# A two-layer trunk on one Trainium2 core: four block products of the up projection in wide matmuls, one more low part by DMA, and another order in the tail

## The chip, the cores and the metric

The kernel runs on one core of one Trainium2 chip. The metric is the device time of one execution in microseconds (us). A core has TensorE (PE, the matrix unit; PEld is its weight load), VectorE (DVE), ScalarE (ACT), GpSimd (POOL) and SyncE (SP), each with its own instruction queue that runs in order, and DMA engines that move data beside them. SP issues the loads of the weights; POOL issues the DMAs that add into their destination.

## The reference

The part that matters is the gated ConvFFN, which each of the two layers has. SEQ is 512, D_MODEL 1024, D_FF 2816, all in float32.

```python
def gated_conv_ffn(x, w_gate, w_up, conv_w, conv_b, w_down):
    g = jnp.einsum('bsd,df->bsf', x, w_gate)
    g = causal_dwconv3(g, conv_w) + conv_b
    up = jnp.einsum('bsd,df->bsf', x, w_up)
    return jnp.einsum('bsf,fd->bsd', jax.nn.silu(g) * up, w_down)
...
def reference(x, ...):
    h = x
    for layer in range(DEPTH):
        xn = rms_norm(h, norm_mix[layer])
        ...
        hn = rms_norm(h, norm_ffn[layer])
        h = h + gated_conv_ffn(hn, w_ffn_gate[layer], w_ffn_up[layer], conv_ffn[layer],
                               b_conv_ffn[layer], w_ffn_down[layer])
    return rms_norm(h, final_norm)
```

## The kernel before

**Two parts for each number.** Every float32 operand of a matmul is split into a high part and a low part of a faster matmul type (float32r): high is a copy on ACT, low is the operand minus high. A product takes three matmuls: high times high, high times low, low times high. There are two ways to make a low part. One is a subtraction on DVE (`parts` and `halves`, L150/L151 and L726/L727). The other (`summed`, L140 to L144, and L766 to L768) writes the negated operand with ACT, then has POOL issue a DMA that adds the operand to it, so that DVE is not used.

**The ConvFFN in pairs.** D_FF is 22 tiles of 128 columns. Tiles 0 and 1 are computed directly; then come ten pairs, f = 2, 4, ..., 20, in each of the two layers (`hidden`, `steps`, STEPS). The pair's gate (g) and up (u) projections are each a 2x2 block product of weights (halves of D_MODEL by two tiles) and activations (halves of the sequence), done in seven block products in place of eight. `prepare(f)` makes the weight sums and splits them: s12 (for products 5 and 6), s34 (for 7 and 3), the plain blocks for 1, 2 and 4. `products(f)` then runs the fourteen block products in the order g1, u1, g5, g2, g6, u5, u6, u2, g7, u7, g3, u3, g4, u4, and takes each result out of PSUM in `after`. Each of g and u has three PSUM banks in a pair: "a" for products 1, 6, 7 and 4 in turn, "e" for 5 and 3, "b" for 2 (BANK). A bank takes the next product only when the one before it has been read.

**Narrow and wide products.** A block product is 128 weight columns by 256 positions over 512 inputs (four steps `kp`). Narrow (L577): twelve matmuls of 256 columns, three a step, all into the left half of the bank. Wide (L567 and L570): high and low part of the activations lie side by side, four matmuls of 512 columns multiply the weight's high part with both at once, so that the low part's share lands in the bank's right half; four of 256 columns then add the weight's low part to the left half. The result is the sum of the two halves. `after` copies the left half with ACT (L806) and adds the right half on DVE (`add`, L794), or adds both halves on DVE where it accumulates. FIRST_WIDE is 6: for f = 6 to 20 all g products and u products 2, 5 and 3 are wide. `in_both` decides it.

**Down projection.** Between the pairs runs the down projection of earlier tiles (`half_down`, matmuls at L155 to L157), whose weights `parts` splits (whi_d on ACT, wlo_d on DVE in layer 0, whi_dn and wlo_dn in layer 1). In layer 1, the last four tiles (18 to 21) go through seven block products of their own, the tail: `block` splits activation blocks into `hg` buffers (high on ACT L1229/L1233, low on DVE L1230/L1234), `put` splits weights, `product` runs the matmuls (L1272) and `taken` adds the result to the output rows y on DVE (L1172). There products 1, 6, 7 (and 4) share a bank, "a", with one bank for each of two row blocks i: `taken(6, 0)` cannot start its matmuls before the addition of `taken(1, 0)` has read that bank.

**What sets the order.** The kernel is traced in program order and a scheduler orders the instructions of each engine by its own estimates, but `behind(x, y)` puts x after y, and `inorder` keeps those instructions that it marks in program order. Buffers of a pool are taken in turn, so an instruction can also wait for the last reader of the buffer that it is about to overwrite.

Of the kernel before, what the change touches and what calls it, by code (L numbers as in the profile page):

```python
# [8 lines left out]
F32 = mybir.dt.float32  # L9
# [22 lines left out]
def tile_trunk(ctx: ExitStack, tc: tile.TileContext, x, norm_mix, norm_ffn, final_norm,  # L32
# [555 lines left out]
    class Ffn:  # L588
# [140 lines left out]
        def prepare(self, f):  # L729

            layer, ap, n = self.layer, self.ap, f"{self.layer}_{f}"
            raws = ffn_weights(layer, f, [(key, half) for half in range(2) for key in "gu"])
            stat = {}

            def put(key, product, hi_lo, i):
                stat[key, product] = hi_lo[0][:, i], hi_lo[1][:, i]

            w = self.unit(f"a11_{n}")
            for i, key in enumerate("gu"):
                self.halves(w[0][:, i], w[1][:, i], raws[key, 0][0][:, :, :P])  # L740
                put(key, 1, w, i)
            for key in "gu":
                r0, r1 = raws[key, 0][0], raws[key, 1][0]
                s12, s34 = (ap.tile([P, 2, 4, P], F32, tag="sum", bufs=3, name=f"{x}{key}_{n}")
                            for x in ("s12", "s34"))
                behind(nc.vector.tensor_tensor(s12[:, 0], r0[:, :, P:], r1[:, :, P:], ALU.add),
                       self.added[key])
                nc.vector.tensor_tensor(s12[:, 1], s12[:, 0], r0[:, :, :P], ALU.subtract)
                w = self.unit(f"s12{key}_{n}")

                def split_s12():
                    self.halves(*w, s12)

                hi, lo = summed(*raws[key, 1], between=split_s12,
                                after=self.first_sums if f == 2 else None)
                put(key, 5, w, 0)
                put(key, 6, w, 1)
                behind(nc.vector.tensor_tensor(s34[:, 0], r0[:, :, :P], r0[:, :, P:],
                                               ALU.subtract), self.added[key])
                nc.vector.tensor_tensor(s34[:, 1], r1[:, :, :P], s12[:, 1], ALU.subtract)  # L760
                for i, product in enumerate((2, 4)):
                    c = slice(i * P, (i + 1) * P)
                    stat[key, product] = hi[:, :, c], lo[:, :, c]
                w = self.unit(f"s34{key}_{n}")
                if key == "g" and f >= FIRST_WIDE:
                    nc.scalar.activation(w[1], s34, AF.Copy, scale=-1.0)  # L766
                    nc.gpsimd.dma_start(w[1], s34, accum_op=ALU.add)
                    nc.scalar.activation(w[0], s34, AF.Copy)  # L768
                else:
                    self.halves(*w, s34)  # L770
                put(key, 7, w, 0)
                put(key, 3, w, 1)
            return stat

        def products(self, f, stat):

            layer, ap, n = self.layer, self.ap, f"{self.layer}_{f}"
            banks = {"g": {}, "u": {}}
            kept = ap.tile([P, 3, HALF], F32, tag="kept", bufs=1, name=f"kept{n}")
            pads = [padded_tile() for _ in range(2)]  # L780
            lo, hi = slice(2, 2 + HALF), slice(2 + HALF, 2 + S)
            dst = {("g", 1): pads[0][:, lo], ("g", 6): pads[0][:, hi], ("g", 7): pads[1][:, hi],
                   ("g", 4): pads[1][:, lo]}
            dst.update({("u", product): kept[:, i, :] for i, product in enumerate((1, 6, 7))})
            onto = {2: 1, 7: 7, 3: 6}
            s = {}

            def in_both(key, product):
                return f >= FIRST_WIDE and (key == "g" or product in (2, 5, 3))

            def add(d, bank, halves):
                ins = None
                for half in halves:
                    ins = nc.vector.tensor_tensor(d, bank[:, half * HALF : (half + 1) * HALF], d,  # L794
                                                  ALU.add)
                return ins

            def after(key, product, bank):
                halves = range(1 + in_both(key, product))
                if product in onto:  # L800
                    ins = add(dst[key, onto[product]], bank, halves)
                    if product == 7:
                        self.added[key] = ins
                elif (key, product) != ("u", 4):
                    d = dst[key, 7 if product == 5 else product]
                    nc.scalar.copy(d, bank[:, :HALF])  # L806
                    add(d, bank, halves[1:])

            for key, product in (("g", 1), ("u", 1), ("g", 5), ("g", 2), ("g", 6), ("u", 5),
                                 ("u", 6), ("u", 2), ("g", 7), ("u", 7), ("g", 3), ("u", 3),  # L810
                                 ("g", 4), ("u", 4)):
                bank = self.multiply(banks[key], f"{key}{n}", product, stat[key, product],
                                     in_both(key, product))
                after(key, product, bank)
                if (key, product) in (("g", 4), ("g", 3)):
                    j = product == 4
                    row = pads[j][:, 2:]
                    nc.vector.tensor_tensor(row, row, self.r, ALU.mult)  # L818
                    s[j] = self.silu(self.conv(pads[j], f + j), f + j)
                    if j and layer == 0:  # L820
                        nc.vector.tensor_tensor(s[1], s[1], self.r, ALU.mult)
            nc.vector.tensor_tensor(s[1][:, HALF:], kept[:, 2, :], s[1][:, HALF:], ALU.mult)
            nc.vector.tensor_tensor(s[1][:, :HALF], bank, s[1][:, :HALF], ALU.mult)
            if layer == 0:
                nc.vector.tensor_tensor(kept[:, :2, :], kept[:, :2, :],
                                        self.r.rearrange("p (a b) -> p a b", a=2), ALU.mult)
            s0 = s[0].rearrange("p (a b) -> p a b", a=2)
            nc.vector.tensor_tensor(s0, kept[:, :2, :], s0, ALU.mult)
            return [(f + 1, s[1]), (f, s[0])]

        def hidden(self, f, before=lambda i, j: None):
# [312 lines left out]
    def ffn1(norm):  # L1144
        with tc.tile_pool(name="f1", bufs=1) as ap:
# [56 lines left out]
            t1, t2 = (ap.tile([P, 2, S], F32, tag="sum", bufs=3, name=f"dnt{i}") for i in (1, 2))  # L1202
            stat = {}

            def put(product, how, src):
                stat[product] = how(src, 2, 512, f"dnp{product}")

            def less(dst, x, y_):
                behind(nc.vector.tensor_tensor(dst, x, y_, ALU.subtract), ffn.added["u"])
# [8 lines left out]
            put(3, summed, b22)  # L1218
            put(7, summed, b12)
            less(b21, b21, t2)  # L1220
            put(4, summed, b21)

            blocks = {}

            def block(product, n, srcs):
                hi, lo = (x.rearrange("p (a b) -> p a b", a=2) for x in hg[n])
                blocks[product] = hi, lo
                if not isinstance(srcs, list):
                    nc.scalar.activation(hi, srcs, AF.Copy)  # L1229
                    nc.vector.tensor_tensor(lo, srcs, hi.bitcast(F32), ALU.subtract)  # L1230
                    return None
                for i, src in enumerate(srcs):
                    ins = nc.scalar.activation(hi[:, i], src, AF.Copy)  # L1233
                    nc.vector.tensor_tensor(lo[:, i], src, hi[:, i].bitcast(F32), ALU.subtract)  # L1234
                return ins

            a11, a12 = ([rows[a + 2 * i + n][:, :HALF] for n in range(2)] for i in range(2))
# [6 lines left out]
            block(5, 4, s1)  # L1244
            for n in range(2):
                nc.vector.tensor_tensor(s2[:, n], s1[:, n], a11[n], ALU.subtract)
            block(6, 5, s2)
            for n in range(2):
                nc.vector.tensor_tensor(a12[n], a12[n], s2[:, n], ALU.subtract)
            last_split = block(3, 6, a12)  # L1250
            for n in range(2):
                nc.vector.tensor_tensor(a21[n], a11[n], a21[n], ALU.subtract)
            block(7, 2, a21)
            block(4, 3, a22)

            first_root = work("sd", 1, "first")
            behind(nc.scalar.activation(first_root, eps, AF.Sqrt), last_split)
            banks = {}

            def product(p, i, c0=0, c1=512, bank=None):  # L1260
# [8 lines left out]
                for k in range(2):  # L1269
                    for l, r, end in ((l_hi, r_hi, False), (l_hi, r_lo, False),  # L1270
                                      (l_lo, r_hi, k == 1)):
                        nc.tensor.matmul(ps, l[:, k, cs], r[:, k, c0:c1], start=first, stop=end,  # L1272
                                         skip_group_check=True)
                        first = False
                return ps

# [4 lines left out]
            def taken(p, i, cs, bank=None):  # L1281

                t = i + 2 * (p in (5, 7, 4))
                part = cs if bank else slice(0, 512)
                inorder(add(y[t][:, cs], product(p, i, part.start, part.stop, bank), t))

            def squared(t, cs):
                sq = tp.tile([P, S], F32, tag="sq", name=f"sqf{t}_{cs.start}")
# [25 lines left out]
                queue.dma_start(out[t * P : (t + 1) * P, cs], dst)  # L1314


            taken(1, 0, left)
            taken(1, 1, left)
            taken(2, 0, left)
            taken(5, 0, right)  # L1320
# [92 lines left out]
```

## Time and profile before

| | us |
|---|---|
| runs | 978.46 to 979.29, median 979.26 |
| profiled execution, its own time | 978.92 |
| its span, first to last instruction | 977.2 |
| busy PE, DVE, ACT, POOL | 966.7, 808.6, 575.6, 130.7 |

The profile is one execution, recorded by the hardware. A page gives busy times and shares of the span, the span in 40 slices (each digit is a share in tenths, PEclk is the granted clock of TensorE), and the chain of work that ended last. A row of a timeline has the start in us, the time that its instructions took together, engine, line, operation, output and inputs by the program's names, the shape, the count, and, in brackets, how long the engine sat idle before it and what ended that. Instructions of one engine overlap at their ends, so a step is read from start to start.

### The profile page before, as it was taken

The numbers are of one execution on the slowest core, as the hardware profiler recorded it, in microseconds if no ns is written. First come the engines' busy times: TensorE is split into PE (matmuls) and PEld (weight loads), VectorE is DVE, ScalarE is ACT, GpSimd is POOL, SyncE is SP. The second block draws the span as 40 slices with busy tenths as digits, with TensorE's granted clock in tenths as the row PEclk, the third lists the DMA queues.
The fourth block names the chain that finished last, engine by engine and source line by source line (L and its number), as shares of the span: only waits on it lengthen the run. The fifth ranks groups of instructions, "written<-read, shape, count | busy, mean of one in ns | idle before, by whom it ended". The sixth has DMA issues, their size and how long they took to land.

```text
span 977.2 us, 14496 instructions
## 1 busy us (share of the span) xinstructions
PE 966.7 (99%) x5456; PEld 845.6 (87%) x5456; DVE 808.6 (83%) x1331; ACT 575.6 (59%) x867; POOL 130.7 (13%) x151
## 2 busy tenths in 40 slices
PE   9999999999999999999999999999999999999996
PEld 7888888998888888888889988889988888888885
DVE  5887459999899898998887765499998979888887
ACT  5523347675565565654588734586665566555675
POOL 2141023010011000110310001310110011000122
PEclk9999999999999999999999999999999999999998
DMA  7442226555666475664324523265656566565674
GB/s 250 146 138 86 87 87 135 138 151 160 153 165 156 119 185 151 159 161 135 114 58 132 195 66 105 55 142 137 177 148 163 152 159 160 142 166 151 174 158 121
DMA packets 91249, 137.63 MB, mean 141 GB/s; under 512 B 4804, under 2 KB 59820, under 8 KB 91180
## 3 DMA queue, kind: packets, MB, share of 16 engines
q1 hardware_dynamic: 78316, 98.69, 30.8%
q0 software_dynamic: 11088, 36.18, 20.9%
q10 hardware_dynamic: 1776, 1.84, 0.6%
q8 instruction: 43, 0.70, 0.3%
q14 instruction: 26, 0.21, 0.1%
HBM read 98.42 MB, written 2.10 MB: 103 GB/s over the span
## 4 chain that ended last, share of the span: by engine, by line
PE 97%; DVE 2%; issue 0%; DMA 0%; ACT 0%; POOLq 0%; DVEq 0%; POOL 0%
PE d L155 3%; PE d L156 3%; PE d L157 3%; PE dn L155 3%; PE dn L156 3%; PE dn L157 3%; PE gu L155 2%; PE gu L157 1%; PE oo L157 1%; PE oo L156 1%; PE gu L156 1%; PE oe L157 1%; PE oe L155 1%; PE oo L155 1%; PE oe L156 1%; PE u_4a L577 1%
## 5 line engine op out<-in xcount | busy, mean ns | idle before, releaser
L612 DVE SCALAR_TENSOR_TENSOR c<-rows,prm,c 128x512 f32<-128x512 f32 x88 | 65.4, 746 | 0.7 <-ACT c L610 0.7
L142 POOL DMA_DIRECT2D wlo_g<-raw_g x20 | 17.2, 862 | 336.6 <-ACT rows L806 242.0
L155 PE MATMUL d<-a_hi,whi_d 128*128 128x512 f32 x144 | 56.1, 390 | 0.0
L155 PE MATMUL dn<-whi_dn,a_hi 128*128 128x512 f32 x144 | 56.1, 390 | 0.0
L156 PE MATMUL d<-a_lo,whi_d 128*128 128x512 f32 x144 | 56.1, 390 | 0.0
L156 PE MATMUL dn<-wlo_dn,a_hi 128*128 128x512 f32 x144 | 56.1, 390 | 0.0
L157 PE MATMUL d<-a_hi,wlo_d 128*128 128x512 f32 x144 | 56.0, 389 | 0.0
L157 PE MATMUL dn<-whi_dn,a_lo 128*128 128x512 f32 x144 | 56.0, 389 | 0.0
L620 ACT ACTIVATE s<-c,prm 128x512 f32<-128x512 f32 x44 | 31.6, 722 | 30.4 <-DVE c L612 30.4
L726 ACT ACTIVATE whi_a<-raw_g 128x512 fp32r<-128x512 f32 x20 | 12.6, 631 | 57.3 <-PE g_6e L567 7.9
L610 ACT ACTIVATE c<-rows,prm 128x512 f32<-128x512 f32 x44 | 31.6, 720 | 11.7 <-DVE rows L818 11.7
L211 POOL TENSOR_TENSOR ssq_f<-ssq_f,sq_f 128x512 f32<-128x512 f32 x14 | 19.8, 1412 | 135.4 <-ACT sq_f L210 100.5
L200 ACT ACTIVATE hg<-h,prm 128x512 fp32r<-128x512 f32 x24 | 17.3, 722 | 32.1 <-DVE h L313 32.1
L727 DVE TENSOR_TENSOR wlo_s34u<-s34u,whi_s34u 128x1024 fp32r<-128x1024 f32 x20 | 24.5, 1225 | 12.7 <-ACT whi_s34u L726 7.4
L151 DVE TENSOR_TENSOR wlo_dn<-raw_dn,whi_dn 128x1024 fp32r<-128x1024 f32 x18 | 22.0, 1224 | 14.2 <-ACT whi_dn L150 14.0
L151 DVE TENSOR_TENSOR wlo_d<-raw_d,whi_d 128x1024 fp32r<-128x1024 f32 x18 | 22.0, 1224 | 13.8 <-ACT whi_d L150 13.8
L157 PEld LDWEIGHTS dn<-whi_dn,a_lo 128*128 128x128 f32 x144 | 27.0, 188 | 5.7
L157 PEld LDWEIGHTS d<-a_hi,wlo_d 128*128 128x128 f32 x144 | 27.0, 188 | 5.7
L726 ACT ACTIVATE whi_s12g<-s12g 128x1024 fp32r<-128x1024 f32 x20 | 21.2, 1061 | 18.0 <-PE g_4e L577 8.7
L201 DVE SCALAR_TENSOR_TENSOR hg<-h,prm,hg 128x512 fp32r<-128x512 f32 x24 | 22.1, 921 | 11.7 <-ACT hg L200 11.7
L155 PEld LDWEIGHTS d<-a_hi,whi_d 128*128 128x128 f32 x144 | 27.1, 188 | 5.4
L155 PEld LDWEIGHTS dn<-whi_dn,a_hi 128*128 128x128 f32 x144 | 27.1, 188 | 5.3
(1125 smaller groups left out, 3398.7 us busy)
## 6 DMA issues: line engine op xcount, KB each, us to landing
raw_g<-in_w_ffn_gate_dram SPq DMA_DIRECT2D x40, 512.0 KB, 4.4
raw_u<-in_w_ffn_up_dram SPq DMA_DIRECT2D x40, 512.0 KB, 3.6
raw_dn<-in_w_ffn_down_dram SPq DMA_DIRECT2D x22, 512.0 KB, 3.6
wlo_u<-raw_u POOLq DMA_DIRECT2D x21, 512.0 KB, 7.2
wlo_g<-raw_g POOLq DMA_DIRECT2D x20, 512.0 KB, 4.7
raw_d<-in_w_ffn_down_dram SPq DMA_DIRECT2D x18, 512.0 KB, 3.5
wlo_s34g<-s34g POOLq DMA_DIRECT2D x16, 512.0 KB, 5.9
raw_oe<-in_w_out_even_dram SPq DMA_DIRECT2D x8, 512.0 KB, 3.5
```

Source lines behind the costliest of these rows:

```text
L151: behind(nc.vector.tensor_tensor(lo, raw, hi.bitcast(F32), ALU.subtract), after[0])
L155: nc.tensor.matmul(ps, lhs[0], rhs[0], start=start, stop=False)
L156: nc.tensor.matmul(ps, lhs[0], rhs[1], start=False, stop=False)
L157: nc.tensor.matmul(ps, lhs[1], rhs[0], start=False, stop=stop)
L200: nc.scalar.activation(hg[k][0], h[k], AF.Copy, scale=g)
L201: nc.vector.scalar_tensor_tensor(hg[k][1], h[k], g, hg[k][0].bitcast(F32), op0=ALU.mult, op1=ALU.subtract)
L211: nc.gpsimd.tensor_tensor(self.ssq, self.ssq, sq, ALU.add)
L610: nc.scalar.activation(c, t[:, 0:S], AF.Copy, scale=prm("cf", ft))
L612: nc.vector.scalar_tensor_tensor(c, t[:, i : S + i], prm("cf", i * NF + ft), c, op0=ALU.mult, op1=ALU.add)
L620: nc.scalar.activation(s, c, AF.Silu, bias=self.prm("bf", ft))
L726: nc.scalar.activation(hi, src, AF.Copy)
L727: nc.vector.tensor_tensor(lo, src, hi.bitcast(F32), ALU.subtract)
```

## The change

Three things change.

All u products of the pairs f = 6 to 20 are wide, as g's were: `in_both` no longer looks at key and product. Products 1, 6, 7 and 4 of u so get a right half that has to be added: for 1, 6 and 7 after the copy or with the accumulation, for 4 by a copy into `kept[:, 0]` and an addition, ahead of the final multiplication, which moves behind the one for s[0].

The low part of s12 for g in the same pairs is made by negated copy and DMA, as s34's was, in place of a subtraction on DVE (`split`).

In the tail of layer 1 the addition of the first product (`first_add`) stands in program order ahead of the blocks 3, 7 and 4, whose low splits are put behind it; the weight split of product 4 comes behind block 6; and the matmuls of `product` are kept in program order.

```diff
+                by_dma = key == "g" and f >= FIRST_WIDE
+
+                def split(w, src):
+                    if not by_dma:
+                        return self.halves(*w, src)
+                    nc.scalar.activation(w[1], src, AF.Copy, scale=-1.0)
+                    nc.gpsimd.dma_start(w[1], src, accum_op=ALU.add)
+                    nc.scalar.activation(w[0], src, AF.Copy)
+
                 def split_s12():
-                    self.halves(*w, s12)
+                    split(w, s12)
...
-                if key == "g" and f >= FIRST_WIDE:
-                    nc.scalar.activation(w[1], s34, AF.Copy, scale=-1.0)
-                    nc.gpsimd.dma_start(w[1], s34, accum_op=ALU.add)
-                    nc.scalar.activation(w[0], s34, AF.Copy)
-                else:
-                    self.halves(*w, s34)
+                split(w, s34)
...
             def in_both(key, product):
-                return f >= FIRST_WIDE and (key == "g" or product in (2, 5, 3))
+                return f >= FIRST_WIDE
...
-            nc.vector.tensor_tensor(s[1][:, HALF:], kept[:, 2, :], s[1][:, HALF:], ALU.mult)
-            nc.vector.tensor_tensor(s[1][:, :HALF], bank, s[1][:, :HALF], ALU.mult)
             if layer == 0:
                 nc.vector.tensor_tensor(kept[:, :2, :], kept[:, :2, :],
                                         self.r.rearrange("p (a b) -> p a b", a=2), ALU.mult)
             s0 = s[0].rearrange("p (a b) -> p a b", a=2)
             nc.vector.tensor_tensor(s0, kept[:, :2, :], s0, ALU.mult)
+            nc.vector.tensor_tensor(s[1][:, HALF:], kept[:, 2, :], s[1][:, HALF:], ALU.mult)
+            last = bank[:, :HALF]
+            if in_both("u", 4):
+                last = kept[:, 0, :]
+                nc.scalar.copy(last, bank[:, :HALF])
+                add(last, bank, (1,))
+            nc.vector.tensor_tensor(s[1][:, :HALF], last, s[1][:, :HALF], ALU.mult)
...
-            put(4, summed, b21)
...
-            def block(product, n, srcs):
+            def block(product, n, srcs, after=None):
...
-                    nc.vector.tensor_tensor(lo[:, i], src, hi[:, i].bitcast(F32), ALU.subtract)
+                    behind(nc.vector.tensor_tensor(lo[:, i], src, hi[:, i].bitcast(F32),
+                                                   ALU.subtract), after)
...
-            block(6, 5, s2)
-            for n in range(2):
-                nc.vector.tensor_tensor(a12[n], a12[n], s2[:, n], ALU.subtract)
-            last_split = block(3, 6, a12)
-            for n in range(2):
-                nc.vector.tensor_tensor(a21[n], a11[n], a21[n], ALU.subtract)
-            block(7, 2, a21)
-            block(4, 3, a22)
-
-            first_root = work("sd", 1, "first")
-            behind(nc.scalar.activation(first_root, eps, AF.Sqrt), last_split)
+            put(4, summed, b21, after=block(6, 5, s2))
...
-                        nc.tensor.matmul(ps, l[:, k, cs], r[:, k, c0:c1], start=first, stop=end,
-                                         skip_group_check=True)
+                        inorder(nc.tensor.matmul(ps, l[:, k, cs], r[:, k, c0:c1], start=first,
+                                                 stop=end, skip_group_check=True))
...
-            taken(1, 0, left)
+            first_add = taken(1, 0, left)
+            for n in range(2):
+                nc.vector.tensor_tensor(a12[n], a12[n], s2[:, n], ALU.subtract)
+            last_split = block(3, 6, a12, first_add)
+            for n in range(2):
+                nc.vector.tensor_tensor(a21[n], a11[n], a21[n], ALU.subtract)
+            block(7, 2, a21, first_add)
+            block(4, 3, a22, first_add)
+
+            first_root = work("sd", 1, "first")
+            behind(nc.scalar.activation(first_root, eps, AF.Sqrt), last_split)
+
             taken(1, 1, left)
```

More of the change, by code (lines that the diff above doesn't have):

```diff
@@ L1203, in ffn1, with put @@
             stat = {}
-            def put(product, how, src):
-                stat[product] = how(src, 2, 512, f"dnp{product}")
+            def put(product, how, src, **kw):
+                stat[product] = how(src, 2, 512, f"dnp{product}", **kw)
             def less(dst, x, y_):
@@ L1228, in block @@
                 if not isinstance(srcs, list):
-                    nc.scalar.activation(hi, srcs, AF.Copy)
-                    nc.vector.tensor_tensor(lo, srcs, hi.bitcast(F32), ALU.subtract)
-                    return None
+                    ins = nc.scalar.activation(hi, srcs, AF.Copy)
+                    behind(nc.vector.tensor_tensor(lo, srcs, hi.bitcast(F32), ALU.subtract), after)
+                    return ins
                 for i, src in enumerate(srcs):
                     ins = nc.scalar.activation(hi[:, i], src, AF.Copy)
-                    nc.vector.tensor_tensor(lo[:, i], src, hi[:, i].bitcast(F32), ALU.subtract)
+                    behind(nc.vector.tensor_tensor(lo[:, i], src, hi[:, i].bitcast(F32),
+                                                   ALU.subtract), after)
                 return ins
@@ L1284, in taken @@
                 part = cs if bank else slice(0, 512)
-                inorder(add(y[t][:, cs], product(p, i, part.start, part.stop, bank), t))
+                return inorder(add(y[t][:, cs], product(p, i, part.start, part.stop, bank), t))
             def squared(t, cs):
```

## The prediction

> **What bounds the kernel now.** I read the page's shares and clock first, then the waits of TensorE, then the chain of waits.
>
> ```profile
> span 977.2 us, 14496 instructions
> ...
> PE 966.7 (99%) x5456; PEld 845.6 (87%) x5456; DVE 808.6 (83%) x1331; ACT 575.6 (59%) x867; POOL 130.7 (13%) x151
> ...
> PEclk9999999999999999999999999999999999999998
> ...
> PE 97%; DVE 2%; issue 0%; DMA 0%; ACT 0%; POOLq 0%; DVEq 0%; POOL 0%
> ...
> PE clock L61 <- DVE idle L56: 1.3, 1, 1.3
> PE dn_a L1272 <- DVE y L1172: 0.8, 1, 0.8
> ```
>
> TensorE is busy for 99% of the span at the full clock, 97% of the ending chain is its own, and it waits twice in all: once at the start and once, for 0.8 us, in the last matmul group. So a gain can come from fewer or shorter matmuls or from that one wait, and a loss from any wait that the change creates on TensorE; work on other engines costs nothing as long as it ends in time. The next view is the timeline of TensorE in one pair (f = 12, layer 0), with narrow products (L577) among wide ones (L567 and L570).
>
> ```profile
> 314.09 1.09 PE L567 MATMUL g_12e<-t,whi_s12g 128*128 128x512 f32 x4
> ...
> 316.90 1.09 PE L567 MATMUL g_12a<-t,whi_s12g 128*128 128x512 f32 x4
> 317.83 0.63 PE L570 MATMUL g_12a<-t,wlo_s12g 128*128 128x256 f32 x4
> 318.30 1.09 PE L567 MATMUL u_12e<-t,whi_s12u 128*128 128x512 f32 x4
> ...
> 319.71 0.40 PE L577 MATMUL u_12a<-t,whi_s12u 128*128 128x256 f32 x2
> ...
> 321.15 1.09 PE L567 MATMUL u_12b<-hg,whi_u 128*128 128x512 f32 x4
> ...
> 323.95 0.40 PE L577 MATMUL u_12a<-t,whi_s34u 128*128 128x256 f32 x2
> ...
> 325.39 0.86 PE L567 MATMUL g_12e<-hg,whi_s34g 128*128 128x512 f32 x3
> ```
>
> Starts are the number to read, since matmuls overlap. Four wide products lie between 314.09 and 319.71, 1.405 us each; two between 321.15 and 323.95, 1.40 each. The two narrow ones take 1.44 each (319.71 to 321.15, 323.95 to 325.39).
>
> **Part 1: the last four narrow products of u become wide.** Each loses eight matmuls of 256 columns and gains four of 512. A product goes from 1.44 to 1.405 us, 0.035 less; f = 6 to 20 in two layers are 16 pairs with four such products, so 64 products: 64 x 0.035 = 2.24 us, which I take as 2.2. The starts are printed to 0.01 us, so the saving is 0.030 to 0.040 and the term 1.9 to 2.6. As TensorE has no gap there, all of it is on the path.
>
> The rows put the fixed part of a matmul at about 9 ns (0.035 over the four fewer matmuls). The Trainium skill (TensorE: Matmul & The Clock Gate, "Wait — 56ns, not 53.3ns?") gives a warm matmul its columns at 2.4 GHz plus about 2.5 ns, which by an estimate from that page would make 256 fewer matmuls worth only 0.64 us. The trace differs: its wide products' first four matmuls are 0.93 us (316.90 to 317.83), 232 ns each, not the 216 ns of that rule, and the sum above goes by the rows.
>
> **What part 1 adds elsewhere.** The result now lies in both halves of its bank, so each product needs one more addition on VectorE (as the 256-column additions below), 4 a pair, and u4 one more ACT copy besides.
>
> ```profile
> 248.80:279.80 31.00, 31.00 (x179) 27.31 (x178) 26.79 (x48) 17.37 (x27) 1.72 (x2) 1.00 0.57 139
> 279.80:310.80 31.00, 31.00 (x179) 27.31 (x178) 29.27 (x52) 19.61 (x28) 3.48 (x5) 1.00 0.67 173
> ...
> 318.03 1.06 ACT L150 ACTIVATE whi_d<-raw_d 128x1024 fp32r<-128x1024 f32 x1 [1.91 <-PE g_12a L567]
> ...
> 321.28 1.06 ACT L150 ACTIVATE whi_d<-raw_d 128x1024 fp32r<-128x1024 f32 x1 [1.00 <-PE u_12a L577]
> 322.24 0.36 ACT L806 COPY kept<-u_12a 128x256 f32<-128x256 f32 x1
> ...
> 319.12 1.23 DVE L151 TENSOR_TENSOR wlo_d<-raw_d,whi_d 128x1024 fp32r<-128x1024 f32 x1 [1.11 <-ACT whi_d L150]
> 320.26 0.42 DVE L794 TENSOR_TENSOR rows<-g_12a,rows 128x256 f32<-128x256 f32 x1
> ```
>
> The first two rows are stretches of one pair each (PE, PEld, DVE, ACT, POOL in that order). VectorE has 1.7 to 4.2 us free in 31; four additions at 0.34 us from start to start (955.13 to 956.13 holds three, in the tail's rows below) are 1.36, of which part 2 gives back 1.14 (319.12 to 320.26, the step of a 128x1024 operation). So VectorE carries about 0.2 us more, ACT about 1.3 more of its 17 to 20, and neither becomes the bound. What counts is when each addition ends, since the next product in the same bank starts with it. In bank "a" of u the order is 1, 6, 7, 4. Products 1 to 6 and 7 to 4 are some four products or more apart; from 6 to 7 only u2 and g7 lie between, and in 14 of the 16 pairs the new addition of u6 stands on VectorE behind wlo_d, which waits for whi_d on ACT.
>
> With S the start of u6: whi_d takes the buffer that u6's high weights leave, and can start when the wide matmuls have read them. After g_12a's that was 318.03 - 316.90 = 1.13 after the start. wlo_d follows 1.09 later (319.12 - 318.03), the addition 1.14 after that, and it takes 0.42: S + 3.78. A matmul that waits for VectorE starts about 0.14 after the result, by the tail's wait (954.47 + 0.75 = 955.22, start 955.36): S + 3.92. By itself u7 starts three wide products after S: S + 4.21. So 0.29 us are left, and I cost this at nothing. The cover is u2 and g7; if it doesn't do, every us of lateness costs 14 us, since g3, u3 and the rest queue behind u7 on TensorE. The bounds: at best nothing, at worst whi_d is released only at the product's end, as in the narrow row (321.28, 1.57 after 319.71; 0.44 later than assumed), so u7 is 0.15 late: 14 x 0.15 = 2.1 us.
>
> For u4 the copy and addition (0.36 and 0.42) lie ahead of its final multiplication; its bank is next used in the pair after, and the down matmuls of its rows come a pair later. Nothing.
>
> **Part 2: the low part of s12 of g by DMA, 16 times.**
>
> ```profile
> L727 DVE TENSOR_TENSOR wlo_s12g<-s12g,whi_s12g x20: 1217/1218/1224, 161.4 to 909.0; 128x1024 fp32r<-128x1024 f32 x20
> ...
> L142 POOL DMA_DIRECT2D wlo_g<-raw_g x20 | 17.2, 862 | 336.6 <-ACT rows L806 242.0
> ...
> wlo_u<-raw_u POOLq DMA_DIRECT2D x21, 512.0 KB, 7.2
> ...
> wlo_s34g<-s34g POOLq DMA_DIRECT2D x16, 512.0 KB, 5.9
> ...
> 243.67 1.22 DVE L727 TENSOR_TENSOR wlo_s12g<-s12g,whi_s12g 128x1024 fp32r<-128x1024 f32 x1
> ...
> 247.53 0.86 POOL L767 DMA_DIRECT2D wlo_s34g<-s34g  x1 [8.39 <-ACT wlo_s34g L766]
> ...
> 253.69 0.63 PE L570 MATMUL g_8e<-t,wlo_s12g 128*128 128x256 f32 x4
> ```
>
> Each takes a subtraction of 1.22 us off VectorE, and adds a negated copy of that shape on ACT (1.06 as whi_d), 0.86 us on POOL, and a transfer of 512 KB that the rows let land 5.9 to 7.2 us after issue. The pair f = 8 is tight, since there s12g is finished late, about where the subtraction stood (243.67): copy until 245.4, POOL issues by 246.3, ahead of s34g's; it lands by 252.2 to 253.5 at 5.9 to 7.2. The first reader is the L570 row at 253.69, so 0.2 to 1.5 us are left. The s34g transfer and the wlo_u one behind it on POOL move back by at most 0.86 each, and POOL is busy 2 to 3.5 us of 31. Cost taken: nothing; bound: 1 us in each layer's f = 8, so 2 us.
>
> **Part 3: the tail.**
>
> ```profile
> 947.95 2.72 DVE L1172 SCALAR_TENSOR_TENSOR y<-dn,small,y 128x512 f32<-128x512 f32 x4
> ...
> 953.46 1.09 DVE L1234 TENSOR_TENSOR hg<-s,hg 128x256 fp32r<-128x256 f32 x3
> 954.47 0.75 DVE L1172 SCALAR_TENSOR_TENSOR y<-dn_a,small,y 128x512 f32<-128x512 f32 x1
> 955.13 1.09 DVE L1234 TENSOR_TENSOR hg<-s,hg 128x256 fp32r<-128x256 f32 x3
> 956.13 0.75 DVE L1172 SCALAR_TENSOR_TENSOR y<-dn_a,small,y 128x512 f32<-128x512 f32 x1
> ...
> 969.84 0.47 DVE L1172 SCALAR_TENSOR_TENSOR y<-dn_d,small,y 128x256 f32<-128x256 f32 x1
> ...
> 952.54 0.39 PE L1272 MATMUL dn_e<-whi_dnp,hg 128*128 128x512 f32 x1
> ...
> 955.36 0.47 PE L1272 MATMUL dn_a<-whi_dnp,hg 128*128 128x512 f32 x1 [0.85 <-DVE y L1172]
> ...
> 957.04 0.40 PE L1272 MATMUL dn_a<-whi_dnp,hg 128*128 128x512 f32 x1
> ...
> 968.62 0.28 PE L1272 MATMUL dn_d<-whi_dnp,hg 128*128 128x256 f32 x1
> ```
>
> Product 6 reuses the bank of product 1, so its first row block (955.36) waits for the addition at 954.47, which stood behind three low splits (953.46, 1.01 us). The new order puts that addition ahead of all six splits. It gains 1.01, loses 0.34 to u4's new addition earlier on the same engine, and comes at about 953.80; the matmul follows 0.89 later (955.36 - 954.47): 954.69. But the six splits now stand between it and the next addition (956.13): 953.80 + 0.66 + 6 x 0.335 = 956.47, and 6,1 starts at 957.36 in place of 957.04, 0.32 later. TensorE also loses what it pulled forward: three dn_e matmuls (two ahead of 955.36, one ahead of 957.04), 0.68 us at 0.227 each, which are now in program order. It ends 1.0 later, at 969.90. The output needs less than that: before, the last matmul ended at 968.90 but the last addition started only at 969.84, since VectorE had those of 3,1 and c before it. Now 3,1 comes ahead of c and d, and the last addition starts at 969.90 + 0.14 = 970.04, which is 0.2 later. Taken: +0.2. Bounds: -0.85, if the wait disappears and nothing comes in its place, and +1.0, if the end follows TensorE.
>
> **Sum.** -2.2 + 0 + 0 + 0.2 = -2.0 us. The profiled execution took 978.92 us (span 977.2 and 1.72 around it), so 976.9; the median of the runs shown, 979.26, stands 0.34 above it, so 977.2.
>
> **The rivals.** *The tail pays too.* The 0.85 us wait goes and the later splits are done before 6,1 asks. For: the addition really stood behind unrelated work. Against: the same splits meet the second addition. 979.26 - 2.2 - 0.85 = 976.2. *Nothing measurable.* The saving on TensorE is lost to its equal: the tail's +1.0 and the f = 8 transfers (up to 2) and give 978.2 to 979.2; or a wide product saves only 0.01 us and 64 of them 0.64 (the page's rule above), which gives 978.8 with the tail at +0.2. For: f = 8 has as little as 0.2 us to spare. Against: wide and narrow products stand side by side in one trace, both without gaps, and differ by 0.035. *Slower.* u7 waits for u6's second half behind wlo_d. It decides from 0.29 us of lateness in the addition; one more 128x256 operation (0.34) together with the late release of 0.44 makes u7 late by 0.49 in 14 pairs: 6.9 us, 977.2 + 6.9 = 984.1; with the late release alone 979.3. For: VectorE is busy 29.3 of 31 us in every second pair, and the wait is new. Against: VectorE sat idle for 1.1 to 1.35 us just before wlo_d, so nothing is piled up there.
>
> **How the numbers follow.** Forecast 0.58, with an own range of 976.2 to 978.2 (the 1.9 to 2.6 of part 1 and half of the tail's bounds); the tail pays too 0.10; nothing 0.09; slower 0.23. A measurement of this kernel tells about 0.2% from no change, 1.96 us, so faster means below 977.3 and slower above 981.2. The forecast lies on that line: 0.38 of its chance counts as faster and 0.20 as same. With 0.10 faster is 0.48; same is 0.20 + 0.09 + 0.01 = 0.30; slower 0.22. The range runs from 975.6, below which some 0.04 remain, to 982.0, which takes in the smaller stalls of u7 and leaves about 0.15 above.
>
> **What would show it.** Right: no L577 rows in the pairs from f = 6 on, products of 1.40 us throughout, no wait of TensorE in the pairs, a wait of about 0.8 us at 6,0 and a new one of about 1.3 at 6,1. Wrong: rows of u7 waiting for VectorE's kept additions, g_8e's L570 rows waiting for a transfer, or wide u products longer than 1.41.

## The result and the profile after

The changed kernel takes 982.50 us (median of 6 runs, 981.56 to 984.28), the kernel before 978.84 in the same comparison (6 runs, 978.44 to 979.29): ratio 1.0040, 95% interval 1.0027 to 1.0053. It is 3.7 us slower, where 2.0 us less were forecast, and lies 0.5 us above the range.

The page of the changed kernel, then its waits of TensorE:

```profile
span 980.7 us, 14161 instructions
...
PE 966.7 (99%) x5200; PEld 832.1 (85%) x5200; DVE 815.2 (83%) x1379; ACT 593.8 (61%) x899; POOL 144.3 (15%) x167
...
PE 86%; DVE 5%; DMA 4%; issue 3%; POOL 0%; ACT 0%; POOLq 0%; DVEq 0%; ACTq 0%
DMA wlo_s12g<-s12g 3%; PE d L157 3%; PE d L156 3%; PE d L155 3%; PE dn L156 2%; PE dn L157 2%; PE dn L155 2%; PE gu L155 2%; PE gu L157 1%; PE oo L157 1%; PE gu L156 1%; PE oo L156 1%; PE oe L156 1%; PE oe L155 1%; PE oo L155 1%
```

```profile
PE g_6a L567 <- DVE rows L798: 3.3, 2, 1.8
PE dn_a L1271 <- DVE y L1181: 1.7, 2, 1.0
PE clock L61 <- DVE idle L56: 1.3, 1, 1.3
PE u_6e L570 <- DVE wlo_s12u L727: 0.2, 1, 0.2
```

The 256 fewer matmuls are there (5456 to 5200), and the busy shares look as before. The chain of waits is what changed: TensorE had 97% of it and has 86%, and a transfer that was not in the kernel before, wlo_s12g, now heads the list by line. The waits say where it comes out: twice at g6 of the pair f = 6, once in each layer. No row names u7.

How far the changed kernel is behind the kernel before, from the starts of the same product in both timelines of TensorE (start after minus start before):

| product | layer 0, us | layer 1, us |
|---|---|---|
| g1 of f = 6 | 0.16 | 2.51 |
| u6 of f = 6 | 2.69 | 4.20 |
| u6 of f = 8 | 2.91 | 4.07 |
| u6 of f = 10 | 3.07 | 3.95 |
| u6 of f = 14 | 2.95 | 3.71 |
| u6 of f = 20 | 2.71 | 3.35 |
| last product, f = 20 | 2.64 | 3.28 |

Pair f = 6 loses 2.5 us in layer 0 and 1.7 in layer 1; f = 8 and 10 of layer 0 lose 0.2 each, net. All other pairs of layer 1 gain 0.12 us each (4.07 at f = 8 to 3.35 at f = 20, six pairs), which is 0.03 a product. The spans differ by 3.5, so what follows the last product, the tail above all, adds 0.2.

VectorE in f = 6 of layer 0, first before, then after:

```profile
211.77 1.22 DVE L727 TENSOR_TENSOR wlo_s12g<-s12g,whi_s12g 128x1024 fp32r<-128x1024 f32 x1
...
223.96 0.69 DVE L758 TENSOR_TENSOR s34u<-raw_u 128x512 f32<-128x512 f32 x1
...
225.17 0.42 DVE L794 TENSOR_TENSOR rows<-g_6a,rows 128x256 f32<-128x256 f32 x1
```

```profile
220.15 0.69 DVE L767 TENSOR_TENSOR s34u<-raw_u 128x512 f32<-128x512 f32 x1 [2.63 <-DMA wlo_s12g<-s12g]
...
221.42 1.88 DVE L313 TENSOR_TENSOR h<-d,h 128x512 f32<-128x512 f32 x3
...
225.09 1.22 DVE L727 TENSOR_TENSOR wlo_s12u<-s12u,whi_s12u 128x1024 fp32r<-128x1024 f32 x1
...
227.42 0.68 DVE L769 TENSOR_TENSOR s34u<-raw_u,s12u 128x512 f32<-128x512 f32 x1
228.02 0.42 DVE L798 TENSOR_TENSOR rows<-g_6a,rows 128x256 f32<-128x256 f32 x1
```

The transfer as the chain of waits has it (start, length), and TensorE at g6:

```profile
213.00 7.12 DMA wlo_s12g<-s12g
```

```profile
228.59 1.15 PE L567 MATMUL g_6a<-t,whi_s12g 128*128 128x512 f32 x4 [1.85 <-DVE rows L798]
```

s34u does not read wlo_s12g, so why does it wait for that transfer? A pair makes four weight sums in program order, s12g, s34g, s12u, s34u, and they share three buffers ("sum", `bufs=3`): the fourth takes the first one's. Before, the last reader of s12g was the subtraction that ended at 212.99. Now it is the DMA, issued at 213.00 and landed 7.12 us later, at 220.12, and s34u starts at 220.15; for so long the transfer holds the buffer. The scheduler had also moved that instruction: in the kernel before it stood behind s12u's split (223.96), now it stands ahead of the additions to h. So VectorE stood for 2.63 us with the rest of its queue behind it, the addition of g1's second half too (228.02, 225.17 before), and g6 needs that bank.

In layer 1 the order was not changed. There s34u stood ahead of the additions (to y, in that layer) in the kernel before as well, and waited for nothing; in the changed kernel, second row below, the same instruction waits for the transfer:

```profile
699.29 0.69 DVE L758 TENSOR_TENSOR s34u<-raw_u 128x512 f32<-128x512 f32 x1
```

```profile
705.51 0.69 DVE L767 TENSOR_TENSOR s34u<-raw_u 128x512 f32<-128x512 f32 x1 [1.78 <-DMA wlo_s12g<-s12g]
```

### The profile page after: what moved, and what is told of

It is laid out like the page before. It is cut to its first block, busy times and chain, and to the rows that moved or that the text cites. A ratio compares the mean times of both kernels' runs of the same rounds, so it can differ in the third digit from the quotient of the medians.

```text
span 980.7 us, 14161 instructions
## 1 busy us (share of the span) xinstructions
PE 966.7 (99%) x5200; PEld 832.1 (85%) x5200; DVE 815.2 (83%) x1379; ACT 593.8 (61%) x899; POOL 144.3 (15%) x167
## 4 chain that ended last, share of the span: by engine, by line
PE 86%; DVE 5%; DMA 4%; issue 3%; POOL 0%; ACT 0%; POOLq 0%; DVEq 0%; ACTq 0%
DMA wlo_s12g<-s12g 3%; PE d L157 3%; PE d L156 3%; PE d L155 3%; PE dn L156 2%; PE dn L157 2%; PE dn L155 2%; PE gu L155 2%; PE gu L157 1%; PE oo L157 1%; PE gu L156 1%; PE oo L156 1%; PE oe L156 1%; PE oe L155 1%; PE oo L155 1%
## 5 line engine op out<-in xcount | busy, mean ns | idle before, releaser
L156 PEld LDWEIGHTS dn<-wlo_dn,a_hi 128*128 128x128 f32 x144 | 27.0, 188 | 5.4
L156 PEld LDWEIGHTS d<-a_lo,whi_d 128*128 128x128 f32 x144 | 27.0, 188 | 5.4
L264 ACT ACTIVATE a_hi<-s 128x512 fp32r<-128x512 f32 x40 | 24.8, 627 | 10.8 <-PE d L157 7.2
```

The source lines that it names most:

```text
L156: nc.tensor.matmul(ps, lhs[0], rhs[1], start=False, stop=False)
L264: nc.scalar.activation(hi, src, AF.Copy, scale=scale)
```

## The experiments

Each kernel was timed beside the kernel before. Theory A is the buffer as just read: source held by the transfer, s34u in front of the queue. Theory B is that f = 6 has too many additions.

**The transfer alone (dma_only).** The kernel before with `split` as in the change (negated copy and DMA for g in f = 6 to 20) and this edit:

```diff
-                    self.halves(*w, s12)
+                    split(w, s12)
```

> The kernel before with one part of the change: the low part of s12 for g by DMA in the 16 wide pairs. Theory A (buffer): s34u takes over the buffer of s12g (four such tiles in a pair, three buffers), and the transfer that now reads s12g holds it until it lands, about 7 us after issue; VectorE stands at s34u for 1 to 2.6 us, and in both pairs f = 6 what is queued behind reaches TensorE, 1.9 to 2.4 us each. Expected 979 + 4 = about 983, with waits of TensorE at g6 of f = 6. Theory B (more additions on VectorE make the addition of g1 late in f = 6): these additions aren't here and a subtraction is gone, so 978.5 to 979.3 and no wait at g6.

Measured: 983.73 us, ratio 1.0048 (1.0036 to 1.0061). Its longest wait of TensorE, and VectorE's on the transfer:

```profile
PE g_6a L567 <- DVE rows L798: 3.2, 2, 1.7
```

```profile
DVE s34u L767 <- DMA wlo_s12g<-s12g: 15.4, 9, 3.0
```

A transfer meant to relieve VectorE costs 4.6 us by itself. VectorE waits for it in nine pairs, 15.4 us in all, but by the starts TensorE is put back in the pairs only in f = 6 of layer 0 (0.20 to 1.97 us behind the kernel before) and of layer 1 (2.01 to 3.94). That is 3.7 of the 4.3 us by which the spans differ; 0.2 were lost before the pairs and some 0.35 come in the tail. Elsewhere VectorE catches up before a product needs it. Theory B falls: there is no additional addition here.

**The wide products alone (wide_only).** The changed kernel with this edit, and the tail of the kernel before:

```diff
-                    split(w, s12)
+                    self.halves(*w, s12)
```

> The kernel before with one part of the change: all u products wide in f = 6 to 20, with the additions and u4's copy; s12 of g split by subtraction as before, tail as before. Theory A: 64 products at 0.035 us less, 978.8 - 2.2 = 976.6, no wait of TensorE in the pairs. Theory B: the wait at g6 of f = 6 is here too, about 3.3 us, 978.8 - 2.2 + 3.3 = 980 or more. A wait at u7 behind wlo_d would show in the later pairs instead, up to 7 us.

Measured: 999.87 us, ratio 1.0213 (1.0194 to 1.0231). Neither theory had this: 21 us slower. The longest wait of TensorE:

```profile
PE u_10b L570 <- DMA wlo_u<-raw_u: 4.7, 2, 4.6
```

and its timeline in f = 10 of layer 0:

```profile
287.68 0.40 PE L567 MATMUL u_10b<-hg,whi_u 128*128 128x512 f32 x1
...
288.46 0.86 PE L567 MATMUL u_10b<-hg,whi_u 128*128 128x512 f32 x3
293.89 0.39 PE L570 MATMUL u_10b<-hg,wlo_u 128*128 128x256 f32 x1 [4.57 <-DMA wlo_u<-raw_u]
```

u2 (u_10b) runs here straight after u5, ahead of u6, so it asks for its low weights a product earlier than in program order. That suggested theory C: the order is at fault. It was tried by itself. (The transfer of these weights was late too: POOL issued it at 285.92, at 281.92 in the kernel before.)

**The wide products alone, matmuls in program order (wide_only_in_order).** As wide_only, and:

```diff
-                nc.tensor.matmul(banks[at], left(kp)[0], both(kp), ...)
+                inorder(nc.tensor.matmul(banks[at], left(kp)[0], both(kp), ...))
...
-                nc.tensor.matmul(ps, left(kp)[1], right(kp)[0], ...)
+                inorder(nc.tensor.matmul(ps, left(kp)[1], right(kp)[0], ...))
```

> The kernel with only the wide part of the change, as in wide_only, and the matmuls of the wide pairs kept in program order. Theory C (wide_only lost its 20.8 us because the scheduler pulled u2 ahead of u6, and u2's low weights come by a transfer that had not landed): the waits at u2 go, 976.6 to 980. Theory D (four more additions a pair are too much for VectorE unless a subtraction leaves it): over 985, with waits for the additions at products of bank a.

Measured: 997.94 us, ratio 1.0200 (1.0187 to 1.0214). Theory C falls: by the medians the order gives back 1.5 of 20.8 us, and the two intervals overlap. Most of the waits moved to where theory D has them:

```profile
PE g_20a L567 <- DVE rows L798: 2.7, 1, 2.7
PE u_18a L567 <- DVE kept L798: 1.8, 2, 1.5
PE u_14a L567 <- DVE kept L798: 1.5, 1, 1.5
PE u_10a L567 <- DVE kept L798: 1.5, 1, 1.5
...
PE u_10b L570 <- DMA wlo_u<-raw_u: 1.0, 1, 1.0
```

In layer 0, f = 10, 14 and 18 lose 3.4 to 4.7 us each by the starts, the pairs between them 0.2; layer 1 gains until f = 18 and loses 4.4 in f = 20. Those three are every second pair, of the kind in which VectorE was busy 29.3 of 31 us before. VectorE in f = 10 there:

```profile
287.40 1.23 DVE L727 TENSOR_TENSOR wlo_s12u<-s12u,whi_s12u 128x1024 fp32r<-128x1024 f32 x1
289.30 1.23 DVE L727 TENSOR_TENSOR wlo_s34u<-s34u,whi_s34u 128x1024 fp32r<-128x1024 f32 x1 [0.67 <-ACT whi_s34u L726]
290.44 0.42 DVE L798 TENSOR_TENSOR kept<-u_10a,kept 128x256 f32<-128x256 f32 x1
```

The new addition of u1 (290.44) stands behind two splits, and u6 waits for it. In the changed kernel, which has part 2 as well, none of these waits is listed. That the subtraction's time on VectorE makes this difference fits the busy rows, but is not shown: no run changed VectorE's load alone, or only the place of this addition, and the waits of 1.0 us at u2 for a transfer are not an addition's.

**The tail alone (tail_only).** The kernel before with the four tail edits of the change.

> The kernel before with one part of the change: the tail. Both theories: 978.8 + 0.2 = 979.0, TensorE waits 0.8 to 1.0 us at 6,0 and again 0.8 to 1.3 us at 6,1. If the tail were the cause of the loss, 981 or more.

Measured: 978.79 us, ratio 0.9998 (0.9989 to 1.0007). No difference, with two waits in place of one, of up to 1.0 us:

```profile
PE dn_a L1262 <- DVE y L1172: 1.3, 2, 1.0
```

The tail is not the cause.

**The transfer from f = 8 on (dma_from_8).** The changed kernel with f = 6 split by subtraction:

```diff
-                    split(w, s12)
+                    (split if f > FIRST_WIDE else lambda w, s: self.halves(*w, s))(w, s12)
```

> The changed kernel, but the low part of s12 for g by DMA only from f = 8 on; f = 6 by subtraction. Theory A: the two waits at g6 of f = 6 (3.3 us, with what they delay 4.2 to 4.5) go, 982.5 - 4.3 = 978.2; what is left above 977 lies in f = 8 and 10 of layer 0. Theory B: 982.5, with the waits at g6 as they were.

Measured: 978.36 us, ratio 0.9995 (0.9986 to 1.0004), as theory A has it. But its waits are not those of the changed kernel with f = 6 cut out:

```profile
PE g_10a L567 <- DVE rows L798: 1.1, 1, 1.1
PE g_8a L567 <- DVE rows L798: 0.2, 1, 0.2
```

VectorE still waits for the transfer in six pairs from f = 8 on, 7.3 us in all. With TensorE 2.5 us earlier and VectorE only 1.4, the addition for g6 of f = 10 in layer 0 comes late and costs some 1.3 us by the starts, against 0.3 in the changed kernel. The stall in f = 6 had covered part of a backlog.

**A buffer of its own (four_buffers), and its control (small_tiles_three).** The changed kernel with four buffers; the room comes from scratch tiles of 16 columns in place of 64 and two others that were cut to size. The control has the smaller tiles and three buffers.

```diff
-                s12, s34 = (ap.tile([P, 2, 4, P], F32, tag="sum", bufs=3, ...
+                s12, s34 = (ap.tile([P, 2, 4, P], F32, tag="sum", bufs=4, ...
...
-        r = tp.tile([P, LINE], F32, tag="rc", name=f"rc_{name}")[:, :n]
+        r = tp.tile([P, PAD], F32, tag="rc", name=f"rc_{name}")[:, :n]
```

> The changed kernel with four buffers in place of three for the weight sums (the room comes from smaller scratch tiles), so s34u has a buffer that no transfer reads. Theory A (buffer): VectorE no longer waits for the transfer of s12g at s34u, the waits of TensorE at g6 of f = 6 go in both layers, 982.5 - 4.2 = 978.3. Rival (the transfers or the extra copies on ACT themselves delay the addition of g1): the waits stay, 982.5.

> Control for four_buffers: the changed kernel with the same smaller scratch tiles, but three buffers. If the smaller tiles shift the other tiles and that alone makes matmuls slower (in four_buffers no wait was left in the pairs, but the 432 dn matmuls came every 0.232 us in place of 0.227 and mixer 0 was 2 us longer), this kernel has both losses: 982.5 + 4 = 986 to 987, with the waits at g6 of f = 6. If four buffers cost something themselves, it is at 982.5 with dn at 0.227.

Measured: four_buffers 982.21 us, ratio 1.0036 (1.0024 to 1.0049), not the 978.3 expected; the control 986.94, ratio 1.0080 (1.0067 to 1.0092), where it was expected. First the waits of TensorE of four_buffers, all of them, then the longest of the control:

```profile
PE clock L61 <- DVE idle L56: 1.3, 1, 1.3
PE dn_a L1271 <- DVE y L1181: 1.0, 1, 1.0
```

```profile
PE g_6a L567 <- DVE rows L798: 2.5, 2, 1.3
```

Behind the kernel before, each in its own comparison, the control is 8.0 us and four_buffers 3.5, so the fourth buffer is worth 4.5 us (3.1 between the two profiled executions), and it takes every wait of TensorE out of the pairs, which is theory A. In f = 6 of layer 0 s34u now runs without a wait although it still stands ahead of the additions to h, 4.2 us before the transfer lands (issued at 215.12, 6.5 us):

```profile
217.40 0.68 DVE L767 TENSOR_TENSOR s34u<-raw_u 128x512 f32<-128x512 f32 x1
```

The smaller tiles cost 4.4 us on their own account (986.94 - 982.50), see the last section.

**s34u later (s34u_later).** The changed kernel with three buffers, and s34u's two subtractions (`first34`, `last34`) behind s12u's split (`low12[-1]`):

```diff
+                if key == "u" and f >= FIRST_WIDE:
+                    behind(first34, low12[-1])
...
+                if key == "u" and f >= FIRST_WIDE:
+                    behind(last34, low12[-1])
```

> The changed kernel with three buffers, but both subtractions of s34u put behind the split of s12u on VectorE in f = 6 to 20, so that the additions to h or y and s12u's split do not stand behind the wait for the transfer. Theory A: the transfer has nearly landed when s34u comes, 978 to 979, with no wait at g6 of f = 6 above 0.5 us. Rival: 982.5.

Measured: 977.39 us, ratio 0.9986 (0.9977 to 0.9994), 1.3 us less than the kernel before. VectorE has no wait for the transfer any more, and in f = 6 of layer 0 s34u now comes 3.5 us after it has landed (issued at 213.07, 7.7 us):

```profile
221.96 1.21 DVE L727 TENSOR_TENSOR wlo_s12u<-s12u,whi_s12u 128x1024 fp32r<-128x1024 f32 x1
...
224.30 0.68 DVE L768 TENSOR_TENSOR s34u<-raw_u 128x512 f32<-128x512 f32 x1
...
225.50 0.41 DVE L804 TENSOR_TENSOR rows<-g_6a,rows 128x256 f32<-128x256 f32 x1
```

The transfers, the wide products and the buffers are those of the change. The edit only moves s34u back in VectorE's queue (the scheduler then placed some other instructions otherwise, too), and 5.0 us go with it: 3.7 behind the kernel before, now 1.3 ahead.

Taken together: the old order in layer 1 without the hold costs nothing (the kernel before), a fourth buffer with s34u still ahead costs no wait (four_buffers), and the hold with s34u further back costs none either (s34u_later). The stall needs both, a source that the transfer holds and a first write to it that stands early in the queue.

**Two versions of it.** With the tail of the kernel before (s34u_later_old_tail), and with the first sums for g of the next pair behind u7's additions (`added["g"]` is what they stand behind):

```diff
-                        self.added[key] = ins
+                        self.added["g"] = self.added[key] = ins
```

> s34u_later with the tail of the kernel before. By the working of the prediction the new tail costs 0.2 us: 977.2 against 977.4 for s34u_later; by tail_only it costs nothing or gains 0.3: 977.4 to 977.7. One wait of 0.8 to 1.2 us in the tail instead of two.

> s34u_later, and the first sum of s12 for g of the next pair put behind u7's additions in place of g7's, so that these do not stand behind its wait for weights (0.25 us at u4 of f = 14 in layer 0). Expected 0.3 to 0.5 us less than s34u_later, 977.0, if nothing else becomes late; 978 or more if the next pair's sums then come too late.

Measured: 977.89 us, ratio 0.9990 (0.9981 to 0.9999), and 977.42 us, ratio 0.9985 (0.9976 to 0.9994). All three intervals overlap, so the tail is again worth nothing that was measured; the first one has a single wait in it, of 1.1 us, as expected. The wait of 0.25 us at u4 of f = 14 is gone from the second one's trace, but the 0.3 to 0.5 us expected of that did not show in the median.

## Why the prediction was wrong

**Part 1, the saving: right, at its lower bound.** 0.03 us a product by the starts in layer 1, where 0.035 was taken from 0.030 to 0.040: 64 x 0.03 = 1.9 us. The estimate from the Trainium skill's page (TensorE: Matmul & The Clock Gate, "Wait — 56ns, not 53.3ns?", 2.5 ns a matmul), 0.64 us, does not agree: these runs show 0.03 over four matmuls, 7.5 ns each.

**Part 1, u7: right.** The addition of u6 was to end at S + 3.78 and u7 to start at S + 4.21. In f = 12 of the changed kernel:

```profile
322.65 1.09 PE L567 MATMUL u_12a<-t,whi_s12u 128*128 128x512 f32 x4
...
326.86 1.09 PE L567 MATMUL u_12a<-t,whi_s34u 128*128 128x512 f32 x4
...
326.06 0.42 DVE L798 TENSOR_TENSOR kept<-u_12a,kept 128x256 f32<-128x256 f32 x1
```

The addition ends at 326.48, S + 3.83, and u7 starts at S + 4.21 without a wait. The slower rival was this wait, and it did not come: that the kernel became slower, as this rival said, has another reason. Nor did the other signs of being wrong that the prediction named: g5 of f = 8 does not wait for a transfer, and the three wide products from u6 to u7 above take 1.40 us each, not over 1.41. The wait came at g6 of f = 6, which it did not name.

**Part 2: the step that failed.** "Cost taken: nothing; bound: 1 us in each layer's f = 8, so 2 us." The working followed the transfer's result, wlo_s12g, to its first reader, and there it was right: in f = 8 of layer 0 the transfer was issued at 248.32, landed 7.14 us later, at 255.46, and was first read at 256.25, 0.8 us later (0.2 to 1.5 had been left). It did not follow the transfer's source. It counted the subtraction of 1.22 us as removed and did not ask what had been waiting for that subtraction to end: s12g's buffer, for s34u. The 1.22 us hold became 7.1, and the order of VectorE's queue, in which s34u stands ahead of the additions to h and y, turned it into a stall. dma_only puts it at 4.6 us, s34u_later and the pair of buffer runs remove 5.0 and 4.5. In f = 8 of layer 0, where the reader was in time, VectorE waited 2.13 us for the same hold, and TensorE fell 0.35 behind there. As for the length of the hold, an estimate from the Trainium skill (DMA: Bandwidth & Descriptors, "Anatomy of one DMA — SWDGE (gpsimd) path", 2.0 us plus bytes over 436e3) gives 3.2 us for 512 KB. The trace does not agree: the page of the profile of the changed kernel has a median of 6.8 us, beside other transfers:

```profile
wlo_s12g<-s12g POOLq DMA_DIRECT2D x16, 512.0 KB, 6.8
```

**"About 0.2 us more" on VectorE: right as a sum, not as a margin.** In the stretch of the changed kernel that holds f = 10 of layer 0 VectorE (third of the busy times) is where it was:

```profile
282.00:313.00 31.00, 30.92 (x162) 26.35 (x162) 29.40 (x55) 21.58 (x31) 4.39 (x6) 1.00 0.78 185
```

But part 1 without part 2 loses 19 to 21 us, far from the 2.2 gained that was expected of it. The prediction read VectorE's share as slack; in those pairs an addition that stood behind two splits was late though VectorE had had 1.7 us of 31 free before.

**Part 3: right.** The waits were to be about 0.8 us at 6,0 and 1.3 at 6,1; the changed kernel has:

```profile
957.08 0.74 DVE L1181 SCALAR_TENSOR_TENSOR y<-dn_a,small,y 128x512 f32<-128x512 f32 x1
957.74 2.14 DVE L1242 TENSOR_TENSOR hg<-s,hg 128x256 fp32r<-128x256 f32 x6
959.80 0.74 DVE L1181 SCALAR_TENSOR_TENSOR y<-dn_a,small,y 128x512 f32<-128x512 f32 x1
...
957.97 0.47 PE L1271 MATMUL dn_a<-whi_dnp,hg 128*128 128x512 f32 x1 [0.64 <-DVE y L1181]
...
960.60 0.50 PE L1271 MATMUL dn_a<-whi_dnp,hg 128*128 128x512 f32 x1 [1.02 <-DVE y L1181]
```

The six splits stand between the two additions, as worked out. The waits are 0.64 and 1.02 us, somewhat shorter. Less the 3.28 us by which TensorE was behind, the additions start at 953.80 and 956.52 and the matmuls at 954.69 and 957.32, where 953.80, 956.47, 954.69 and 957.36 were worked out. The tail costs 0.2 us by the spans and nothing that tail_only could measure.

**The sum.** By the table f = 6 cost 4.2 us, the saving is 1.9, the tail 0.2, the slips in f = 8 to 18 of layer 0 some 0.85 (at u6 the seven pairs from f = 8 to 20 lost 0.02 where they should have gained 0.12 each), and 0.15 was lost before the first pair: 4.2 - 1.9 + 0.2 + 0.85 + 0.15 = 3.5, by which the spans differ. Without the stall the kernel gains 1.3 us (s34u_later), where 2.0 were forecast.

## What to carry to other kernels

A DMA that takes over work from an engine also holds the buffers that this work read, for as long as the transfer lasts (7.1 us here, 1.22 before); look for the next tile that gets the source's buffer, not only for the reader of the result. Then look where its first write stands in its engine's queue: a few places later, the same hold costs nothing. And two edits that lean on each other can't be judged one by one: here one alone cost 4.6 us, the other alone 19 to 21, and both together 3.7.

## What was not expected of the hardware

Some matmuls became slower, at the same shape, when small scratch tiles were shortened (by 192 bytes a partition for 48 columns). Other tiles may lie elsewhere in the memory by that; no view shows where. The down matmuls of layer 1 in the list of groups, first of the changed kernel, then of small_tiles_three (one execution each):

```profile
L156 PE MATMUL dn<-wlo_dn,a_hi 128*128 128x512 f32 x144 | 56.2, 390 | 0.0
```

```profile
L156 PE MATMUL dn<-wlo_dn,a_hi 128*128 128x512 f32 x144 | 56.8, 395 | 0.0
```

From start to start it is 0.228 and 0.232 us (means over the dn rows of both timelines; 0.232 in four_buffers too), about 2 us over 432 of them. In four_buffers TensorE was 2.5 us behind the kernel before when the first pair began, from the starts. No wait of TensorE stands against this in the lists above. It is not the clock: the mean granted clock of small_tiles_three is 0.998 (0.997 in the changed kernel), and its down matmuls of layer 0 (tile d), of the same shape, have 0.228 as in the changed kernel. The cause stays open, and which tile's place matters, if it is that, wasn't tried.
